# Buffers, banks and order at the stage borders of an encoder step

## The chip, the cores and the metric

The kernel runs on one core of a Trainium2 chip. The metric is the time of one execution in microseconds (us) on the device; the kernel before took 2932.59 us, the median of three runs (2931.63 to 2932.82). The engines are TensorE (PE, with its weight loads PEld), VectorE (DVE), ScalarE (ACT), GpSimd (POOL) and SyncE (SP), which here only issues DMAs. Each engine works off its own queue of instructions in a fixed order; where an instruction waits, everything behind it in that queue waits too.

## The reference

One layer of a streaming encoder, for a new stream of 2048 frames (16 tiles of 128 rows) and for the next 16 frames of 8 running streams (one more tile, the samples', number 16):

```python
def encoder_layer(x, ...):
    h = rmsnorm(x, g_mix_pre)
    y, new_k, new_v, new_conv = parallel_mixer(h, ...)   # band attention | conv, then w_out
    x = x + rmsnorm(y, g_mix_post)
    h = rmsnorm(x, g_mem_pre)
    x = x + rmsnorm(memory_attention(h, mk, mv, w_mq, w_mo), g_mem_post)
    h = rmsnorm(x, g_ffn_pre)
    f = (silu(h @ w_gate) * (h @ w_up)) @ w_down
    x = x + rmsnorm(f, g_ffn_post)
    return x, new_k, new_v, new_conv
```

The model width is 1024, the hidden width 2816, the memory has 256 tokens. All is fp32.

## The kernel before

Every large product is made of three matmuls on operands split into a high part (a cast to fp32r on ACT) and a low part (a subtraction on DVE or POOL). `mm3` (L271 to L273) does that for one output bank, `mm3h` (L279) for two halves of 512 columns. So each weight tile that is loaded costs an ACT cast and a DVE or POOL subtraction before TensorE can use it.

The stages run one after the other, but the instructions of neighbouring stages are mixed. A planner (the scheduler of the framework, which works with a timeline of its own at build time) writes the order of each engine's queue by the priority of the instructions, which is their order in the program. `high_priority(offset=n)` moves a block n places forward in that order, and `issue_after(ins)` makes those instructions of a block that run on the engine of `ins` come after it in that queue; instructions on other engines are not bound by it.

Memory is laid out by hand. `sbF` (fp32), `sbR` (fp32r, its last 20 KB per partition named `sbx` in the profile) and `ps` (the eight 2 KB banks of PSUM, `psb`) are areas of a fixed size, and `flexb` are pieces that come and go with a stage. A `Region` gives names to places in KB: `lay` puts buffers one behind the other, `at` at given offsets. Each name is a ring: the n-th tile of a name gets place n modulo the number of places. Two stages' names may lie on the same bytes, and then the later one waits until the earlier one's last reader is done.

The stages and what the change touches in them:

- Projection and convolution (`phase_proj`). The last group's norms (`late_norms`, `conv_norm`, L516 to L540) run inside the attention's first steps. Their normalised tile `xnx` lies after `thx` and `zx`, at 28 and 30 KB of `sbF`; the key output `ko` lies at 21 to 29 KB and is stored by L674.
- Attention (`attention`), 128 units of (head, tile). Near its end, `weigh` (L921) turns the row sums of tile 0 and tile 1 into reciprocals and transposes them, at the units named by `WEIGH`; the output weights are loaded by `out_weights`.
- Output projection (`mixout`), 17 tiles in the order samples, 0, 1, ... 15. `by_column(t)` (L935, POOL) spreads tile t's reciprocals into one buffer `rj`; `prep(t)` loads the convolution's part, multiplies with L979 (PE) and L982 (DVE), and splits the result into `mh` and `ml` (L988 ACT, L989 DVE). A tile's product takes 48 matmuls (L1017, helper L279) into two banks of the ring `y`. Then come squares (L1031), the scale (L1032, L288, L289 on POOL), L1035 (DVE, two halves, which frees the two banks and writes `po`), the residual add L1036 (POOL) and the store L1037. The ring `p` of banks serves `prep`, `weigh` and the transposes of the samples' work. That work is the whole memory attention of the samples' tile, a generator `cross_sample` which the loop advances by `RATE` steps after each second k from the tile number `FROM` on; its weights are split by L1075 (ACT) and L1076 (DVE), and it ends with `postnorm` (L324 to L330), which also takes `po`.
- Memory attention (`phase_cross`), 16 tiles: `norm(t)` (load of `xt`, L296, L288, L289, L303, transposes L306, split L307 and L308), `scores(t)` with the eight weights `f1`, softmax (L1209 to L1218), `probs(t)` (transposes L1224, split L1227 and L1228), `values(t)` with the eight weights `f2`, then `postnorm` (L328 on DVE, the add L329 and the store L330 on POOL). The weights go through the staging ring `stg` (`load`, L1188 SP, L1191 ACT, L1192 DVE or POOL). `natural(g, p)` (L1241 to L1264) takes a pair of finished tiles, normalises them (L1252, L1254 and L1255 on POOL, L1256 on DVE), makes sums and differences on POOL (L1257 to L1263) and stores seven forms in DRAM (`hn`). There are nine pairs (`PAIRS`), and the loop does at most one after each tile.
- Gate and up (`gate_up`), three groups of three pairs by 22 blocks of weights. `tform(g, j)` loads form j of a group (L1331, three loads), transposes it (L1334) and splits it (L1336 ACT, L1337 DVE). `wforms(f)` loads gate and up (L1343, L1344), makes sums on POOL (L1351 to L1354) and splits seven forms (L1356 ACT, L1357 DVE). Seven products of 12 matmuls (L1364) make one block. The first `wforms` and the seven first `tform` stand under `high_priority(offset=HP)`. What is left of the pairs is done here, one after each second block of group 0.
- Down (`down`) is not touched.

## Time and profile before

| | us |
|---|---|
| median of three runs | 2932.59 |
| the profiled execution | 2939.42 |
| its span, first to last instruction | 2937.6 |
| DVE busy | 2072.0 |
| ACT busy | 1306.7 |
| POOL busy | 1413.3 |
| transfers: mean over the span | 169 GB/s |

The profile is of one execution. PE's share of the span includes matmuls that ran at a lower clock, so a busy PE is not PE at its best. In a timeline row stand the start, the duration, the engine and line, the operation and its tiles, and in brackets how long the engine was idle before it and which instruction ended the wait. A row of a stretch gives the busy time of each engine with its count of instructions, then the granted clock of TensorE (1.00 is full speed), the share of DMA time and the rate.

### The profile page before, as it was taken

The numbers are of one execution on the slowest core, as the hardware profiler recorded it, in microseconds if no ns is written. First come the engines' busy times: TensorE is split into PE (matmuls) and PEld (weight loads), VectorE is DVE, ScalarE is ACT, GpSimd is POOL, SyncE is SP. The second block draws the span as 40 slices with busy tenths as digits, with TensorE's granted clock in tenths as the row PEclk, the third lists the DMA queues.
The fourth block names the chain that finished last, engine by engine and source line by source line (L and its number), as shares of the span: only waits on it lengthen the run. The fifth ranks groups of instructions, "written<-read, shape, count | busy, mean of one in ns | idle before, by whom it ended". The sixth has DMA issues, their size and how long they took to land.

```text
span 2937.6 us, 44541 instructions
## 1 busy us (share of the span) xinstructions
PE 2873.1 (98%) x16248; PEld 2594.9 (88%) x16248; DVE 2072.0 (71%) x3053; ACT 1306.7 (44%) x2623; POOL 1413.3 (48%) x1298
## 2 busy tenths in 40 slices
PE   9999999999999998999989999999999999999998
PEld 8999999988877677888879999999999998888786
DVE  7696885889983344344568888788788997555656
ACT  4444465678872233232334333433344444332433
POOL 1367496731133443153656555456556775424413
PEclk9999999999999999999999999999999999999999
DMA  8635253666535664132454333644344446656664
GB/s 289 245 106 189 80 179 116 207 225 219 209 116 188 234 209 136 57 132 93 158 181 163 116 134 120 206 161 157 130 150 142 143 143 226 222 172 227 224 216 142
DMA packets 200383, 496.81 MB, mean 169 GB/s; under 512 B 19258, under 2 KB 90810, under 8 KB 191323
## 3 DMA queue, kind: packets, MB, share of 16 engines
q1 hardware_dynamic: 186274, 426.98, 43.3%
q0 software_dynamic: 13888, 66.98, 6.1%
q8 instruction: 127, 2.08, 0.3%
q14 instruction: 94, 0.76, 0.1%
HBM read 362.82 MB, written 139.16 MB: 171 GB/s over the span
## 4 chain that ended last, share of the span: by engine, by line
PE 41%; DMA 4%; POOL 3%; DVE 3%; issue 2%; ACT 0%; SPq 0%; DVEq 0%; POOLq 0%; ACTq 0%
PE psb L273 13%; PE psb L272 13%; PE psb L271 13%; DMA sbf<-in_w_down_dram 2%; PE psb L279 1%; POOL sbf L1479 1%; DMA sbf<-x 1%; PE psb L1334 1%; DMA sbf<-in_w_gate_dram 0%; DVE sbr L1549 0%; DMA sbf<-hn 0%; DVE sbr L1357 0%; POOL sbf L329 0%; DVE sbx L1357 0%; DMA hn<-sbf 0%
## 5 line engine op out<-in xcount | busy, mean ns | idle before, releaser
L271 PE MATMUL psb<-sbr 128*128 128x384 f32 (+3 forms) x2672 | 916.5, 345 | 4.5 <-ACT sbr L1548 1.7
L272 PE MATMUL psb<-sbr 128*128 128x384 f32 (+3 forms) x2356 | 805.2, 342 | 0.5 <-DVE sbr L321 0.3
L273 PE MATMUL psb<-sbr 128*128 128x512 f32 (+2 forms) x1712 | 610.2, 358 | 3.7 <-DVE sbr L1549 3.6
L271 PEld LDWEIGHTS psb<-sbr 128*128 128x128 f32 x2672 | 503.8, 189 | 40.0 <-ACT sbr L1548 3.5
L273 PE MATMUL psb<-sbr,sbx 128*128 128x384 f32 (+2 forms) x1484 | 475.5, 322 | 1.6 <-POOL sbx L266 1.6
L272 PEld LDWEIGHTS psb<-sbr 128*128 128x128 f32 x2356 | 445.3, 189 | 27.4 <-DVE sbr L321 1.0
L273 PEld LDWEIGHTS psb<-sbr 128*128 128x128 f32 x1712 | 322.0, 188 | 39.7 <-DVE sbr L1549 7.5
L1357 DVE TENSOR_TENSOR sbr<-sbf,sbr 128x512 fp32r<-128x512 f32 x258 | 263.1, 1023 | 38.9 <-ACT sbr L1356 38.3
L273 PEld LDWEIGHTS psb<-sbr,sbx 128*128 128x128 f32 x1484 | 280.2, 189 | 1.9 <-POOL sbx L266 1.8
L1356 ACT CAST sbr<-sbf 128x512 fp32r<-128x512 f32 x258 | 159.1, 620 | 275.7 <-PE psb L272 232.2
L504 DVE SCALAR_TENSOR_TENSOR psb<-sbf,psb 128x768 f32<-128x768 f32 (+1 forms) x290 | 264.2, 911 | 6.2
L279 PE MATMUL psb<-sbr 128*128 128x512 f32 x984 | 244.2, 397 | 9.7 <-DVE flexb L1035 7.3
L279 PEld LDWEIGHTS psb<-sbr 128*128 128x128 f32 x984 | 184.0, 190 | 55.0 <-DVE flexb L1035 7.5
L1549 DVE TENSOR_TENSOR sbr<-sbf,sbr 128x384 fp32r<-128x384 f32 (+2 forms) x242 | 165.3, 707 | 93.9 <-ACT sbr L1548 92.9
L266 POOL TENSOR_TENSOR sbx<-sbf,sbr 128x1024 fp32r<-128x1024 f32 (+1 forms) x62 | 151.1, 2440 | 80.4 <-ACT sbr L264 70.5
L279 PE MATMUL psb<-sbr,sbx 128*128 128x512 f32 x750 | 186.7, 396 | 2.7 <-DVE sbx L989 1.8
L1479 POOL TENSOR_TENSOR sbf<-sbf 128x512 f32<-128x512 f32 x77 | 107.0, 1393 | 169.8 <-DMA sbf<-in_w_down_dram 168.1
L1548 ACT CAST sbr<-sbf 128x384 fp32r<-128x384 f32 (+2 forms) x242 | 112.6, 483 | 169.8 <-PE psb L272 145.9
L514 POOL TENSOR_TENSOR flexb<-flexb,flexb 128x128 f32<-128x128 f32 (+1 forms) x180 | 171.2, 952 | 20.5 <-ACT flexb L513 11.1
L271 PE MATMUL psb<-sbr,sbx 128*128 128x384 f32 (+1 forms) x524 | 170.9, 327 | 2.7 <-ACT sbx L1356 1.9
L279 PEld LDWEIGHTS psb<-sbr,sbx 128*128 128x128 f32 x750 | 139.6, 189 | 37.1 <-issue 3.3
L1356 ACT CAST sbx<-sbf 128x512 fp32r<-128x512 f32 x153 | 94.8, 620 | 165.0 <-PE psb L272 142.9
(328 smaller groups left out, 5903.4 us busy)
## 6 DMA issues: line engine op xcount, KB each, us to landing
af<-flexb SPq DMA_DIRECT2D x33, 1344.0 KB, 5.7
sbf<-in_w_down_dram SPq DMA_DIRECT2D x154, 256.0 KB, 3.5
sbf<-in_w_gate_dram SPq DMA_DIRECT2D x66, 512.0 KB, 3.4
sbf<-in_w_up_dram SPq DMA_DIRECT2D x66, 512.0 KB, 3.5
sbf<-af SPq DMA_DIRECT2D x85, 384.0 KB, 4.1
sbf<-x SPq DMA_DIRECT2D x49, 512.0 KB, 4.0
sbf<-in_w_in_dram SPq DMA_DIRECT2D x48, 512.0 KB, 3.9
sbr<-ks POOLq DMA_DIRECT2D x16, 1024.0 KB, 8.6
```

Of the source, the lines that this page charges most:

```text
L266: self.lo_engine.tensor_tensor(lo[:, c], wf[:, c], hi[:, c].bitcast(F32), ALU.subtract)
L271: nc.tensor.matmul(ps, lh, rh, start=start, stop=False, **kw)
L272: nc.tensor.matmul(ps, lh, rl, start=False, stop=False, **kw)
L273: nc.tensor.matmul(ps, ll, rh, start=False, stop=stop, **kw)
L279: nc.tensor.matmul(y[o], l, r[:, o * 512:(o + 1) * 512], start=start and x == 0, stop=stop and x == 2)
L504: nc.vector.scalar_tensor_tensor(acc if w < CW - 1 else o, src(w), cwt[:, j, w:w + 1], acc, ALU.mult, ALU.add)
L514: nc.gpsimd.tensor_tensor(o, o, v, ALU.add)
L1356: nc.scalar.copy(hs[j][:, :], src[j])
L1357: nc.vector.tensor_tensor(ls[j][:, :], src[j], hs[j][:, :].bitcast(F32), ALU.subtract)
L1479: nc.gpsimd.tensor_tensor(acc[:, :], acc[:, :], q[:, :], ALU.add if s > 0 else ALU.subtract)
L1548: nc.scalar.copy(ch[:, m], a[:, x, m])
L1549: nc.vector.tensor_tensor(cl[:, m], a[:, x, m], ch[:, m].bitcast(F32), ALU.subtract)
```

## The change

The diff does the following, border by border.

- Late norms: the two places of `xnx` are used in the reverse order, 30 KB first.
- Attention to output projection: tile 0 and tile 1 are weighed at units 117 and 122 instead of 122 and 124, and `by_column(0)` is done two units after the first, instead of at the start of `mixout`.
- Output projection: `y` has four banks and `p` two, instead of three and three; the samples' `postnorm` gets a buffer of its own, `spo`; `RATE` is 1.5 instead of 1.3; the samples' instructions that run on DVE are put behind the last split that `prep` has written so far.
- Memory attention: the staging ring has four places instead of three for the first twelve weights (eight `f1`, four `f2`), and three (`stg2`) for the rest; four `f2` weights instead of two are written ahead of the rest, now before the first `scores`, and no longer tied to its last exponential. `natural` runs behind the residual add of the same tile on POOL and no longer after the last tile, so that the pair (12, 14) moves into `gate_up`; its buffer `nt` moves to 22 KB there.
- Gate and up: other homes for weights (`wf`), sums (`s`) and loaded forms (`nat`, with nine places `nat0` for group 0 and five for the others instead of three), other homes for forms 4 and 5, another order of the banks for products, four banks instead of two for the transposes of group 0 (`tr0`), and `HP` 300 instead of 100.

```diff
@@ -34,17 +34,17 @@
 KL = PAST + DEC_S - 2 * KB
 EPS = 1e-6
 NEG = -1e30
-RATE = 1.3
+RATE = 1.5
 DEPTH = 2
-WEIGH = (122, 124)
+WEIGH = (117, 122)
 FROM = 2
-F2 = 2
+F2 = 4
 MID = 4
 TR0 = [12, 8]
 MM = [12, 14, 4, 6]
 LATE = 15
 WARM = (6, 0, 6)
-HP = 100
+HP = 300
 HP2 = 200
 
 GROUPS = [[[0, 1, 2], [3, 4, 5]], [[6, 7, 8], [9, 10, 11]], [[12, 13, 14], [15, S_TILE]]]
@@ -172,7 +172,7 @@
                    .at("qhx", 1.5, (fa, [17.5]), (fb, [6]), (sbF, [12, 13.5]))
                    .at("qlx", 1.5, (fa, [19]), (fb, [7.5]), (sbF, [15, 16.5]))
                    .lay(sbF, 18, ("vo", 1, 3), ("ko", 8, 1))
-                   .lay(sbF, 22, ("thx", 2, 1), ("zx", 2, 2), ("xnx", 2, 2))
+                   .lay(sbF, 22, ("thx", 2, 1), ("zx", 2, 2)).at("xnx", 2, (sbF, [30, 28]))
                 .lay(sbF, 44.75, ("us", 5.75, 1), ("cwt", 0.484375, 1), ("cvec", 0.0625, 1), ("half", 0.0625, 1))
                    .lay(fb, 0, ("ct", 3, 5), ("bst", 0.03125, 2), ("bmv", 0.03125, 2), ("ss", 0.03125, 6),
                         ("rstd", 0.03125, 6))
@@ -321,13 +321,14 @@
                     nc.vector.tensor_tensor(lo[:, sl, :], ps[:, :, :], hi[:, sl, :].bitcast(F32), ALU.subtract))
         return last
 
-    def postnorm(self, pool, y, xt, gbc, dst, dma=None, bufs=2):
+    def postnorm(self, pool, y, xt, gbc, dst, tag="po"):
         nc = self.nc
         r = self.rms(pool, y)
-        o = self.t(pool, [P, D], F32, "po", bufs)
+        o = self.t(pool, [P, D], F32, tag)
         nc.vector.scalar_tensor_tensor(o[:, :], y, r[:, :], gbc[:, :], ALU.mult, ALU.mult)
-        nc.gpsimd.tensor_tensor(o[:, :], o[:, :], xt[:, :], ALU.add)
+        added = nc.gpsimd.tensor_tensor(o[:, :], o[:, :], xt[:, :], ALU.add)
         nc.gpsimd.dma_start(dst, o[:, :])
+        return added
 
     def finish(self, pool, y, xt, gbc, dst, parts, engine):
 
@@ -895,6 +896,8 @@
             if i in WEIGH:
                 for _ in self.weigh(WEIGH.index(i), ps_t, "t"):
                     pass
+            if i == WEIGH[0] + 2:
+                self.by_column(0)
             if i in (n - 13, n - 11, n - 9, n - 7):
                 next(self.wo_load)
 
@@ -958,13 +961,13 @@
         sbF, sbR = self.sbF, self.sbR
         (ft, fr), ff = self.flex(ctx, (2048, F32), (2048, F32R)), self.fa
         pool = (Region().lay(sbF, 34.5, ("wf", 4, 3), ("gbc", 4, 1))
-                .at("ct", 2, (ff, [2, 10])).lay(ff, 0, ("an", 2, 1)).lay(ff, 5, ("po", 4, 1))
+                .at("ct", 2, (ff, [2, 10])).lay(ff, 0, ("an", 2, 1)).lay(ff, 5, ("po", 4, 1)).at("spo", 4, (ff, [22]))
                 .lay(ff, 12, ("junk", 2, 1), ("xt", 4, 2), ("sh", 8, 1), ("ss", 0.03125, 6), ("rstd", 0.03125, 6),
                      ("nmx", 0.03125, 1), ("sm", 0.03125, 1), ("ri", 0.03125, 1)).lay(ff, 26, ("sgain", 4, 1))
                 .at("mh", 4, (sbR, [40, 88])).at("ml", 4, (sbR, [44, 92]))
                 .lay(sbR, 96, ("sTh", 4, 1), ("sTl", 4, 1)).lay(ft, 0, ("sT", 8, 1))
                 .at("kvh", 4, (sbR, [64, 80]), (fr, [0])).at("kvl", 4, (sbR, [104, 84]), (fr, [4])))
-        ps_y = ps_p = ps_so = Region().lay(self.ps, 0, ("y", 2, 3), ("p", 2, 3), ("so", 4, 1))
+        ps_y = ps_p = ps_so = Region().lay(self.ps, 0, ("y", 2, 4), ("p", 2, 2), ("so", 4, 1))
         for _ in self.wo_load:
             pass
         ws, self.w = self.wo, pool
@@ -986,7 +989,7 @@
             ml = self.t(pool, [P, KC, P], F32R, "ml", 2)
             for sl, src in ((slice(4, 8), ct[:, :, :]), (slice(0, 4), att)):
                 nc.scalar.copy(mh[:, sl, :], src)
-                nc.vector.tensor_tensor(ml[:, sl, :], src, mh[:, sl, :].bitcast(F32), ALU.subtract)
+                self.last_prep = nc.vector.tensor_tensor(ml[:, sl, :], src, mh[:, sl, :].bitcast(F32), ALU.subtract)
             ready[t] = (mh, ml)
 
         def ahead(i):
@@ -1003,8 +1006,6 @@
         ready = {}
         with self.tc.high_priority(offset=HP2):
             for t in order[:2]:
-                if t != S_TILE:
-                    self.by_column(t)
                 prep(t)
         fill, steps, due = iter(()), 0, 0.0
         for i, t in enumerate(order):
@@ -1019,7 +1020,8 @@
                     next(pre, None)
                     due += RATE if i >= FROM else 0.0
                     while due >= 1:
-                        next(fill, None)
+                        with self.tc.issue_after(self.last_prep.ins):
+                            next(fill, None)
                         due -= 1
             for _ in pre:
                 pass
@@ -1162,13 +1164,14 @@
         yield from dense(oT, "w_mo", y)
         xt = self.t(pool, [P, D], F32, "xt", 2)
         nc.sync.dma_start(xt[:, :], self.x1[S_TILE])
-        self.postnorm(pool, flat(y), xt, gpost, self.x2[S_TILE], bufs=1)
+        self.postnorm(pool, flat(y), xt, gpost, self.x2[S_TILE], "spo")
 
     def phase_cross(self, ctx):
         nc, A = self.nc, self.A
         sbF, sbR = self.sbF, self.sbR
         fr = Joined(*self.flex(ctx, *[(1024, F32R)] * 11))
-        pool = (Region().lay(sbF, 0, ("stg", 4, 3), ("gpre", 4, 1), ("junk", 2, 1), ("hn", 4, 1), ("xt", 4, 3))
+        pool = (Region().lay(sbF, 12, ("gpre", 4, 1), ("junk", 2, 1), ("hn", 4, 1), ("xt", 4, 3))
+                .at("stg", 4, (sbF, [0, 4, 8, 30])).at("stg2", 4, (sbF, [0, 4, 8]))
                 .lay(sbF, 34.5, ("gpost", 4, 1), ("z", 4, 2), ("po", 4, 1), ("ss", 0.015625, 6),
                      ("rstd", 0.015625, 6), ("nmx", 0.03125, 2), ("sm", 0.03125, 2), ("ri", 0.03125, 2))
                 .at("sh", 4, (sbR, [96, 44, 24])).at("sl", 4, (sbR, [100, 52, 28]))
@@ -1183,8 +1186,8 @@
         gpre = self.gain(pool, "g_mem_pre", "gpre")
         gpost = self.gain(pool, "g_mem_post", "gpost")
 
-        def load(src, tag, engine=nc.vector):
-            wf = self.t(pool, [P, D], F32, "stg")
+        def load(src, tag, engine=nc.vector, stage="stg"):
+            wf = self.t(pool, [P, D], F32, stage)
             nc.sync.dma_start(wf[:, :], src)
             wh = self.t(pool, [P, D], F32R, tag + "h", 1)
             wl = self.t(pool, [P, D], F32R, tag + "l", 1)
@@ -1210,8 +1213,8 @@
             z = self.t(pool, [P, MH, NM], F32, "z", 2)
             sm = self.t(pool, [P, MH], F32, "sm", 2)
             for h in range(MH):
-                self.last_exp = nc.scalar.activation(z[:, h, :], sv[:, h, :], AF.Exp, bias=nmx[:, h:h + 1],
-                                                     accum_out=sm[:, h:h + 1])
+                nc.scalar.activation(z[:, h, :], sv[:, h, :], AF.Exp, bias=nmx[:, h:h + 1],
+                                     accum_out=sm[:, h:h + 1])
             ri = self.t(pool, [P, MH], F32, "ri", 2)
             nc.vector.reciprocal(ri[:, :], sm[:, :])
             for h in range(MH):
@@ -1234,7 +1237,7 @@
                 if t == NPT - 2 and k == MID:
                     self.last_probs = probs(z)
                 self.mm3h(halves(y), ph[:, k, :], pl[:, k, :], f2[k][0], f2[k][1], k == 0, k == KC - 1)
-            self.postnorm(pool, y[:, :, :].rearrange("p a b -> p (a b)"), xt, gpost, self.x2[t], bufs=1)
+            return self.postnorm(pool, y[:, :, :].rearrange("p a b -> p (a b)"), xt, gpost, self.x2[t])
 
         gffn = self.gain(Region().at("gffn", 4, (self.gffn, [0])), "g_ffn_pre", "gffn")
 
@@ -1269,30 +1272,26 @@
         f1 = [load(self.f1s[:, k, :, :].rearrange("p h n -> p (h n)"), f"f1{k}",
                    nc.gpsimd if k in (1, 3, 5) else nc.vector) for k in range(KC)]
         hq[1] = norm(1)
+        f2 = [load(self.f2s[:, k, :], f"f2{k}") for k in range(F2)]
         z = scores(*hq[0][1:], "y")
-        f2 = []
-
-        def more(n, event):
-            with self.tc.issue_after(event.ins):
-                for k in range(len(f2), min(len(f2) + n, KC)):
-                    f2.append(load(self.f2s[:, k, :], f"f2{k}"))
-
-        more(F2, self.last_exp)
         for t in range(NPT):
             pp = probs(z) if t < NPT - 1 else self.last_probs
             if t == 0:
-                more(KC, self.last_split)
+                with self.tc.issue_after(self.last_split.ins):
+                    f2 += [load(self.f2s[:, k, :], f"f2{k}", stage="stg2") for k in range(F2, KC)]
             if t + 1 < NPT:
                 z = scores(*hq[t + 1][1:])
             if t + 2 < NPT:
                 hq[t + 2] = norm(t + 2)
-            values(t, hq.pop(t)[0], *pp)
+            added = values(t, hq.pop(t)[0], *pp)
             for g, p in list(todo):
                 ready = all(x == S_TILE or x < t for x, _ in PAIRS[g][p][:2])
-                if ready and t >= 4:
-                    natural(g, p)
+                if ready and 4 <= t < NPT - 1:
+                    with self.tc.issue_after(added.ins):
+                        natural(g, p)
                     todo.remove((g, p))
                     break
+        pool.at("nt", 4, (sbF, [22]))
         self.todo = todo
 
     def shift_caches(self, name, s):
@@ -1310,16 +1309,17 @@
         sbF, sbR = self.sbF, self.sbR
         t6h, t6l, w8, fx, af0, af1 = self.flex(ctx, (1536, F32R), (1536, F32R), (1024, F32R), (1536, F32), (2688, F32),
                                                (2688, F32))
-        pool = (Region().at("wf", 4, (sbF, [12, 18, 46.5, 22]))
-                .at("s", 2, (sbF, [26, 28, 38.5])).at("nat", 2, (sbF, [40.5, 42.5, 44.5]))
+        pool = (Region().at("wf", 4, (sbF, [12, 18, 26, 42.5]))
+                .at("s", 2, (sbF, [8, 10, 38.5])).at("nat", 2, (sbF, [0, 2, 4, 6, 40.5])).at("nat0", 2, (sbF, [0, 2, 4, 6, 40.5, 12, 14, 18, 20]))
                 .at("x1", 1.5, (sbF, [30, 31.5])).at("x2", 1.5, (sbF, [33, 34.5]))
                 .at("x3", 1.5, (sbF, [36]), (fx, [0])).at("th", 1.5, (fx, [1.5, 3, 4.5]))
                 .at("wh", 2, (sbR, [68, 72, 76, 80, 84, 88, 92, 104]), (w8, [0]))
                 .at("wl", 2, (sbR, [70, 74, 78, 82, 86, 90, 94, 106]), (w8, [2]))
                 .at("af", 10.5, (af0, [0]), (af1, [0])).at("t6h", 6, (t6h, [0])).at("t6l", 6, (t6l, [0])))
-        for j, (oh, ol) in enumerate(((0, 6), (12, 18), (56, 62), (24, 30), (36, 42), (48, 96))):
+        for j, (oh, ol) in enumerate(((0, 6), (12, 18), (56, 62), (24, 30), (36, 96), (42, 48))):
             pool.at(f"t{j}h", 6, (sbR, [oh])).at(f"t{j}l", 6, (sbR, [ol]))
-        ps_mm = ps_tr = Region().at("mm", 2, (self.ps, [8, 10, 0, 2, 4, 6])).at("tr", 2, (self.ps, [12, 14]))
+        ps_mm = ps_tr = (Region().at("mm", 2, (self.ps, [0, 2, 4, 6, 8, 10])).at("tr", 2, (self.ps, [12, 14]))
+                         .at("tr0", 2, (self.ps, [12, 14, 8, 10])))
         ts = [None] * 7
 
         def tform(g, j):
@@ -1327,9 +1327,9 @@
             lo = self.t(pool, [P, 4, 3 * P], F32R, f"t{j}l")
             for p in range(3):
                 n = PAIRS[g][p][2]
-                x = self.t(pool, [P, 512], F32, "nat")
+                x = self.t(pool, [P, 512], F32, "nat" if g else "nat0")
                 nc.sync.dma_start(x[:n, :], self.hn[g][:n, p, TFORM[j], :])
-                ps = self.t(ps_tr, [P, 4, P], F32, "tr")
+                ps = self.t(ps_tr, [P, 4, P], F32, "tr" if g else "tr0")
                 for k in range(4):
                     nc.tensor.transpose(ps[:, k, :n], x[:n, k * P:(k + 1) * P], self.ident[:n, :n])
                 c = slice(p * P, p * P + n)
```

## The prediction

> **What bounds the kernel now.** I read the page first, then the busy time by stretches, the list of what TensorE waited for, and the order of time around each place where it stood still.
>
> ```profile
> span 2937.6 us, 44541 instructions
> PE 2873.1 (98%) x16248; PEld 2594.9 (88%) x16248; DVE 2072.0 (71%) x3053; ACT 1306.7 (44%) x2623; POOL 1413.3 (48%) x1298
> ```
>
> TensorE is busy 2873.1 of 2937.6 us, and the change takes no matmul away. It can win only TensorE's idle time and the half-speed matmuls after it. So I looked for both at the borders between stages.
>
> ```profile
> 841.00:876.00 35.00, 30.18 (x161) 24.50 (x160) 27.33 (x45) 20.37 (x41) 11.15 (x10) 0.95 0.46 151
> 1105.00:1112.00 7.00, 0.05 (x1) 0.00 (x0) 1.40 (x2) 1.08 (x2) 5.39 (x7) 0.70 0.43 151
> 1143.00:1149.00 6.00, 4.31 (x26) 3.30 (x25) 5.79 (x6) 3.96 (x11) 0.00 (x0) 1.00 0.55 175
> 1505.00:1520.00 15.00, 10.59 (x65) 8.84 (x63) 11.71 (x13) 8.27 (x16) 11.09 (x12) 1.00 0.73 235
> 1520.00:1532.00 12.00, 7.27 (x35) 5.89 (x35) 3.92 (x8) 3.67 (x7) 5.54 (x7) 0.82 0.75 261
> 1532.00:1538.00 6.00, 6.00 (x19) 6.00 (x20) 4.92 (x6) 2.57 (x5) 5.32 (x5) 0.51 0.42 152
> 1538.00:1544.00 6.00, 6.00 (x39) 5.93 (x39) 4.42 (x6) 2.66 (x5) 4.39 (x3) 1.00 0.57 188
> 1870.00:1880.00 10.00, 7.91 (x51) 7.36 (x50) 6.51 (x12) 4.53 (x8) 3.50 (x3) 1.00 0.72 245
> ...
> 875.00:1105.00 230.00, 230.00 (x1170) 168.96 (x1169) 93.11 (x144) 72.69 (x173) 90.72 (x102) 1.00 0.62 210
> 1150.00:1490.00 340.00, 336.99 (x1595) 280.18 (x1594) 158.22 (x168) 107.08 (x233) 142.20 (x170) 1.00 0.32 110
> ...
> 1540.00:1870.00 330.00, 329.17 (x1921) 328.07 (x1920) 274.85 (x372) 132.81 (x244) 195.81 (x145) 1.00 0.41 145
> ```
>
> The columns are the stretch, its length, the busy time of PE, PEld, DVE, ACT and POOL, the granted clock, DMA share and GB/s. Length less PE is idle: 4.82 into the output projection, 6.95 at its end, 1.69 at the first memory attention, 4.41 + 4.73 = 9.14 into gate and up, 2.09 at its first change of group, 3.01 inside the memory attention, nothing inside the output projection. At 1532 to 1538 the granted clock is 0.51, and 19 matmuls run where 39 run in the next 6 us: about 3 us more.
>
> **The end of the output projection: four "y" banks and the own row buffer.**
>
> ```profile
> 1098.67 5.61 PE L279 MATMUL psb<-sbr 128*128 128x512 f32 x24
> ...
> 1112.32 8.44 PE L279 MATMUL psb<-sbr 128*128 128x512 f32 x24 [7.27 <-DVE flexb L1035]
> ...
> 1104.86 3.25 POOL L329 TENSOR_TENSOR flexb<-flexb 128x1024 f32<-128x1024 f32 x1 [7.84 <-DVE flexb L328]
> ...
> 1108.44 0.63 POOL L330 DMA_DIRECT2D x<-flexb  x1
> ...
> 1111.51 1.41 DVE L1035 SCALAR_TENSOR_TENSOR flexb<-psb,flexb,sbf 128x512 f32<-128x512 f32 x2 [5.60 <-DMA x<-flexb]
> ```
>
> Three banks serve two halves per tile, so the second half of the last tile reuses a bank of the tile before, which L1035 must empty. L1035 writes "po", and that one buffer still holds the samples' row until its store (L330) has left. So TensorE stands 7.27 us, and the 24 matmuls then take 8.44 instead of 5.61: 2.83 more. With four banks the last tile reuses those of two tiles back, and with "spo" L1035 does not wait for the store either. All 7.27 + 2.83 = 10.10 can go. What is late next is the first scores: their weights are split into places that the projection's weights leave, and TensorE comes 10 us sooner.
>
> ```profile
> 1123.95 1.05 ACT L1191 CAST sbr<-sbf 128x1024 fp32r<-128x1024 f32 x1 [0.81 <-DMA sbf<-f1s]
> ```
>
> That split waits for its load. Four staging buffers instead of three bring loads forward, and the freed last tile releases its weights from its first matmuls on. I take 9.0 of 10.1; the bounds are 0 (the loads do not move) and 10.1. The samples' work at RATE 1.5 instead of 1.3 is the same work sooner: nothing, as the stretch from 875 is full.
>
> TensorE's half clock after the pause is a rule of the Trainium skill too (TensorE: Matmul & The Clock Gate, "What's actually happening"): about 3.4 us of idleness halve the clock, about 3.4 us of work restore it. By that each pause would cost 1.7 us beside itself, an estimate; the rows say 2.83 and 3, and they count.
>
> **The start of the memory attention.** Four value weights split before the first softmax, not two behind its exponential, take splits out of the chain. Its 1.69 idle waits for transposed probabilities, which four splits don't shorten, but the scores come apart. I take 0.7, between 0 and 1.7.
>
> **Into gate and up: other homes, priority 300, no 'natural' at the end.**
>
> ```profile
> PE psb L1334 <- DMA sbf<-hn: 4.5, 2, 3.5
> PE psb L271 <- ACT sbx L1356: 1.9, 1, 1.9
> PE psb L1334 <- DVE sbr L1337: 1.8, 3, 1.0
> ...
> 1509.15 3.03 DVE L1256 SCALAR_TENSOR_TENSOR sbf<-sbf,flexb 128x1024 f32<-128x1024 f32 x1
> ...
> 1513.53 9.71 SPq L1331 DMA_DIRECT2D sbf<-hn  x5
> ...
> 1531.24 1.26 POOL L1352 TENSOR_TENSOR sbf<-sbf 128x512 f32<-128x512 f32 x1 [6.44 <-DMA sbf<-in_w_gate_dram]
> ...
> L1337 DVE TENSOR_TENSOR sbr<-psb,sbr 128x512 fp32r<-128x512 f32 x15 | 10.0, 685 | 13.3 <-ACT sbr L1336 13.3
> ```
>
> Three causes, each met by an edit. The 21 loads of the first forms (L1331) go through three buffers that lie on the softmax's tiles: 4.5 us. Nine buffers on the old staging area can be filled before. The second pair of weights (L1352) waits for a home under "po" (46.5) and "xt" (22); the new homes 26 and 42.5 are free earlier: 1.9. The pair (12, 14) of 'natural' stands in DVE's queue between the forms (L1256): 1.8; it moves into gate and up. Form 4 leaves the place of the last probabilities, so only forms 5 and 6 need the last values; they come 60 matmuls in. Idle 9.14 and 3 of slow clock make 12.1, and at 0.82 over 12 us up to 2.2 more: 14.3. I take 12.0, bounds 3 (below) and 14.3.
>
> The price is the pair moved. Its two L1256 and four adds (L1257 to L1263) now meet a stage in which DVE is busy 274.85 of 330 us:
>
> ```profile
> L1256 DVE SCALAR_TENSOR_TENSOR sbf<-sbf,flexb x18: 1276/1284/3417, 1255.9 to 1551.4; 128x1024 f32<-128x1024 f32 x16, 64x1024 f32<-64x1024 f32 x2
> ...
> L1257 POOL TENSOR_TENSOR sbf<-sbf x9: 1255/1285/1665, 1265.6 to 1552.8; 128x512 f32<-128x512 f32 x8, 64x512 f32<-64x512 f32 x1
> ```
>
> That is 2 x 1.28 to 2 x 3.42 on DVE and 4 x 1.29 on POOL, against DVE's idle 55 us in 22 steps, 2.5 each. It is spread over two or three steps; I charge 1.2, bounds 0 and 6.8 (all of the worst on the path).
>
> A rule of the Trainium skill speaks against this move (SBUF — State Buffer, "Who interferes with whom"): a DVE instruction with two SBUF inputs and a GpSimd one that reads SBUF block each other whole. The spread from 1276 to 3417 agrees. By it the four adds hold DVE for 5.2 us beyond its own 2.6, 7.8 as an estimate, and if none of it were covered the sum would lose 6.6 more.
>
> **Into the output projection: (117, 122), the early product of tile 0, DVE order.**
>
> ```profile
> 867.82 1.05 ACT L1075 CAST flexb<-sbf 128x1024 fp32r<-128x1024 f32 x1 [2.85 <-DMA sbf<-in_w_mq_dram]
> ...
> 868.95 1.23 DVE L1076 TENSOR_TENSOR flexb<-sbf,flexb 128x1024 fp32r<-128x1024 f32 x1 [2.24 <-ACT flexb L1075]
> ...
> 872.15 1.28 DVE L989 TENSOR_TENSOR sbx<-flexb,sbx 128x512 fp32r<-128x512 f32 x2
> ...
> 872.89 3.41 PE L279 MATMUL psb<-sbr,sbx 128*128 128x512 f32 x8 [1.76 <-DVE sbx L989]
> ```
>
> Splits of the samples' weights (L1076, two of 1.2 us) stand on DVE before tile 0's (L989), which TensorE waits for. 'issue_after' puts them behind it: 1.76 idle goes, and with it 3.41 - 8 x 5.61/24 = 1.54 of slow matmuls. ACT's cast (L1075) is not moved, so its 2.85 can remain. I take 3.3, bounds 0 and 4.82 + 1.54 = 6.4.
>
> **Smaller places.** The late norms wait for a store of the keys that lies under their buffer; with the order turned the first lies elsewhere:
>
> ```profile
> 614.03 0.81 DVE L528 TENSOR_SCALAR sbf<-psb,flexb 128x512 f32<-128x512 f32 x1 [1.44 <-DMA out_dram<-sbf]
> ...
> PE psb L532 <- DVE sbf L528: 1.6, 1, 1.6
> ```
>
> I take 1.2 of 1.6. Inside the memory attention 'natural' goes ahead of the residual add:
>
> ```profile
> 1302.67 1.28 DVE L328 SCALAR_TENSOR_TENSOR sbf<-psb,sbf 128x1024 f32<-128x1024 f32 x1 [3.33 <-POOL sbf L289]
> ...
> 1307.10 0.19 POOL L1254 TENSOR_SCALAR sbf<-sbf 128x1 f32<-128x1 f32 x1 [4.46 <-ACT sbf L1252]
> ...
> 1307.90 2.39 POOL L329 TENSOR_TENSOR sbf<-sbf 128x1024 f32<-128x1024 f32 x1
> ```
>
> L328 ends at 1303.95, the add starts at 1307.90, and the next norm's "xt" is free only after it. With the add first: 2.0 of the 3.01. The change of group has more load buffers but the same two banks: 0.5 of 2.09.
>
> **Two "p" banks for three.** A bank is held for little more than
>
> ```profile
> L982 DVE TENSOR_TENSOR flexb<-sbf,psb 128x512 f32<-128x512 f32 x15 | 10.2, 683 | 15.3 <-PE psb L979 15.3
> ...
> L979 PE MATMUL psb<-sbr 128*128 128x512 f32 x13 | 5.4, 414 | 0.0
> ```
>
> 0.41 + 0.68 us, a few times in a tile of 15 us. I charge 1.0 in all, bounds 0 and the last rival.
>
> **Sum.** 9.0 + 0.7 + 12.0 + 3.3 + 1.2 + 2.0 + 0.5 - 1.2 - 1.0 = 26.5 us. The profiled execution took 2939.4 (1.8 of it outside the span) and would take 2912.9; the median of the three runs is 6.8 lower, so 2932.6 - 26.5 = 2906.1.
>
> **The rivals.**
> One handover gives nothing. Either the first scores wait for their weights (9.0 back), or priority 300 puts five to nine forms on DVE ahead of the last probabilities: 0.685 each, 3.4 to 6.2, and 3 of clock, up to 9. For it: the split above waits for its load, and 21 forms and 7 splits fill DVE there. Against: four buffers. 2906.1 + 9 = 2915, to 2923 with small losses: 0.20. Both: 2924: 0.08.
> The edits do not reach the chip: instruction order follows the planner's clock, and each wait moves to the next in line. Within 6 us of before, 0.04; against it, the buffers and banks are places, not order.
> Slower: the two "p" banks. Products, weights' turns and the samples' turns share them, and TensorE takes them in order; a third request waits. Without that charge the gain is 27.5, so from 27.5/15 = 1.8 us a tile over 15 tiles it is used up. At 2.5 us, two holds of 1.1 and a queue behind the splits, it is 37.5: 2942.6. For it: the samples' DVE work now stands behind 'prep'. Against: no idle in the 230 us of that stage. 0.07.
> More than forecast, above 35 us: 0.03.
>
> **How the numbers follow.** The forecast, a gain of 18 to 35, has 0.58. The range 2896 to 2922 holds it, most of the 0.20 and a little of the last: 0.8. Faster by over 0.2% (5.9 us, about what a measurement can tell) is 0.58 + 0.20 + 0.03 and 0.05 of the 0.08: 0.86. Same: 0.04 + 0.03 = 0.07. Slower: 0.07.
>
> **What would show it.** The 7.27 before L279 and the clock of 0.51 are gone; L1334 no longer waits for hn; L989 runs before L1076; stretches as long as 1505 to 1538 show no more than 2 us idle. A wait of L279 for L1191/L1192, or idle time inside the output projection at L979 or L1057, would prove me wrong.

## The result, and the profile after

| | median, us | lowest to highest | runs |
|---|---|---|---|
| before | 2932.11 | 2930.31 to 2932.82 | 4 |
| after | 2916.14 | 2912.2 to 2917.7 | 4 |

The ratio is 0.9944, 95% interval [0.9927, 0.9962]: 16 us faster (11 to 21), where 26.5 were forecast. The profiled execution of after took 2912.2 (span 2910.4), the fastest of its four, and that of before 2939.4, 7 above its median; so the two profiles lie 27.2 apart, more than the medians, and places are compared here, not spans.

The page of after, its first lines:

```profile
span 2910.4 us, 44563 instructions
PE 2859.6 (98%) x16248; PEld 2589.3 (89%) x16248; DVE 2081.8 (72%) x3053; ACT 1308.3 (45%) x2623; POOL 1400.0 (48%) x1298
```

Busy time by stretches of after, the columns as in the prediction (stretch, length, PE, PEld, DVE, ACT, POOL, granted clock, DMA share, GB/s):

```profile
839.00:874.00 35.00, 32.32 (x175) 26.48 (x174) 23.58 (x36) 19.95 (x36) 11.54 (x10) 1.00 0.45 143
874.00:1089.00 215.00, 212.69 (x1105) 157.71 (x1104) 90.18 (x140) 68.77 (x164) 84.20 (x102) 0.99 0.64 220
935.00:950.00 15.00, 12.74 (x83) 7.81 (x75) 8.21 (x17) 3.66 (x10) 6.47 (x8) 0.89 0.85 282
1089.00:1104.00 15.00, 15.00 (x72) 12.51 (x71) 13.29 (x10) 7.63 (x11) 11.81 (x8) 1.00 0.64 215
1126.00:1133.00 7.00, 5.12 (x30) 3.84 (x29) 5.55 (x5) 4.25 (x12) 0.75 (x2) 1.00 0.00 0
1133.00:1473.00 340.00, 340.00 (x1620) 283.94 (x1619) 157.92 (x171) 106.84 (x233) 137.23 (x170) 1.00 0.33 114
1473.00:1573.00 100.00, 91.09 (x527) 87.96 (x525) 82.31 (x99) 42.65 (x80) 67.83 (x60) 0.98 0.50 180
1573.00:1820.00 247.00, 247.00 (x1432) 246.90 (x1431) 200.98 (x273) 94.29 (x171) 143.42 (x103) 1.00 0.34 125
1820.00:1850.00 30.00, 29.40 (x186) 27.98 (x185) 24.92 (x39) 16.33 (x32) 11.74 (x10) 1.00 0.72 240
2440.00:2450.00 10.00, 7.44 (x27) 5.67 (x26) 9.84 (x14) 3.77 (x8) 7.22 (x7) 0.83 0.80 254
```

The end of the output projection (1089 to 1104) and the inside of the memory attention (1133 to 1473) are full. Inside the projection 2.3 us of idle time and a clock of 0.89 have come up, at 935 to 950. The first change of group begins at 1812 in a full stretch and has 0.60 idle in 1820 to 1850. Most of what is left stands in 1473 to 1573, the way into gate and up with its first blocks: 8.91 idle, and about 2 us for a clock of 0.98. The list of what TensorE waited for in after (in total, times, the longest) says for what:

```profile
PE psb L271 <- DVE flexb L1407: 6.3, 2, 5.4
...
PE psb L271 <- DVE sbf L1396: 2.3, 1, 2.3
PE psb L1097 <- DMA sbf<-in_cache_mem_kT_dram: 2.3, 3, 1.7
...
PE psb L271 <- DVE sbf L1407: 1.2, 1, 1.2
...
PE psb L533 <- DVE sbf L529: 0.3, 1, 0.3
```

L1334 is gone from it: the first forms no longer wait for their loads. L1396 is new, and L1407 has 6.3 and 1.2 where before had 2.1: DVE empties the banks of the first blocks too late (L1407 also has 0.9 at 2217, outside the border). Into the output projection, and at its end, the timeline of after shows:

```profile
866.73 1.20 PE L279 MATMUL psb<-sbr,sbx 128*128 128x512 f32 x4 [1.36 <-ACT sbx L991]
...
866.97 1.29 DVE L992 TENSOR_TENSOR sbx<-flexb,sbx 128x512 fp32r<-128x512 f32 x2
...
1095.64 8.78 PE L279 MATMUL psb<-sbr 128*128 128x512 f32 x38
```

L992 is the old L989; it now runs ahead of every split of the samples' weights (the old L1076, from 886 on). The product waits 1.36 for the cast instead. At the end 38 matmuls run without a pause.

One place that the change does not touch became longer, the way into down. Before, by stretches:

```profile
2465.00:2480.00 15.00, 12.94 (x60) 10.40 (x59) 13.81 (x20) 5.81 (x13) 9.05 (x8) 1.00 0.80 255
```

2.06 idle at full clock before; 2.56 idle, and 1.7 us for a clock of 0.83, after.

The two executions also differ in clock where no edit explains it. The row of before:

```profile
545.00:625.00 80.00, 75.26 (x473) 71.55 (x471) 65.63 (x119) 48.27 (x128) 49.58 (x76) 0.96 0.75 249
```

The clock of this stretch is 1.00 in after, but 0.98 in the profile of the same kernel run again, and 1.00 in before with only the border of gate and up changed. At 0.96 it costs before about 3 us, so a term read from one execution is good to some 2 or 3 us.

### The profile page after: what moved, and what is told of

The parts are those of the page before. It is cut to its first block, busy times and chain, and to the rows that moved or that the text cites. A ratio compares the mean times of both kernels' runs of the same rounds, so it can differ in the third digit from the quotient of the medians.

```text
span 2910.4 us, 44563 instructions
## 1 busy us (share of the span) xinstructions
PE 2859.6 (98%) x16248; PEld 2589.3 (89%) x16248; DVE 2081.8 (72%) x3053; ACT 1308.3 (45%) x2623; POOL 1400.0 (48%) x1298
## 4 chain that ended last, share of the span: by engine, by line
PE 81%; DVE 5%; DMA 5%; POOL 3%; issue 3%; ACT 2%; SPq 0%; DVEq 0%; POOLq 0%; ACTq 0%
PE psb L273 18%; PE psb L272 18%; PE psb L271 18%; PE psb L279 18%; DMA sbf<-in_w_down_dram 2%; PE psb L848 2%; PE psb L817 2%; PE psb L835 1%; POOL sbf L1479 1%; PE psb L1334 1%; DMA sbf<-x 1%; POOL flexb L515 1%; PE psb L1097 1%; DMA sbf<-in_x_prompt_dram 1%; DVE flexb L732 1%
## 5 line engine op out<-in xcount | busy, mean ns | idle before, releaser
L273 PE MATMUL psb<-sbr 128*128 128x512 f32 (+2 forms) x1712 | 609.1, 357 | 4.7 <-DVE sbr L1549 4.6
L273 PE MATMUL psb<-sbr,sbx 128*128 128x384 f32 (+2 forms) x1484 | 474.5, 321 | 1.6 <-POOL sbx L266 1.6
L273 PEld LDWEIGHTS psb<-sbr 128*128 128x128 f32 x1712 | 321.0, 188 | 40.2 <-DVE sbr L1549 8.2
L1357 DVE TENSOR_TENSOR sbr<-sbf,sbr 128x512 fp32r<-128x512 f32 x258 | 258.1, 1003 | 48.2 <-ACT sbr L1356 45.0
L273 PEld LDWEIGHTS psb<-sbr,sbx 128*128 128x128 f32 x1484 | 279.9, 189 | 1.9 <-POOL sbx L266 1.8
L279 PE MATMUL psb<-sbr 128*128 128x512 f32 x984 | 241.2, 395 | 1.4 <-DVE sbr L266 0.5
L279 PEld LDWEIGHTS psb<-sbr 128*128 128x128 f32 x984 | 182.6, 189 | 45.2 <-issue 4.3
L279 PE MATMUL psb<-sbr,sbx 128*128 128x512 f32 x750 | 184.6, 394 | 1.7 <-ACT sbx L991 1.4
L1357 DVE TENSOR_TENSOR sbx<-sbf,sbx 128x512 fp32r<-128x512 f32 x153 | 165.9, 1087 | 14.9 <-ACT sbx L1356 14.6
L279 PEld LDWEIGHTS psb<-sbr,sbx 128*128 128x128 f32 x750 | 138.7, 188 | 36.0 <-issue 4.5
```

The source lines that it names most:

```text
L273: nc.tensor.matmul(ps, ll, rh, start=False, stop=stop, **kw)
L279: nc.tensor.matmul(y[o], l, r[:, o * 512:(o + 1) * 512], start=start and x == 0, stop=stop and x == 2)
L1357: nc.vector.tensor_tensor(ls[j][:, :], src[j], hs[j][:, :].bitcast(F32), ALU.subtract)
```

## The experiments

All times are medians beside runs of before on the same chip (medians 2936.7 to 2938.2 there), and gains are differences of medians; the intervals are those of the ratio. Eight kernels ran on one chip in two rounds; the two with the adds on DVE and the one with the pair (12, 14) back on a second, the pairs taken apart on a third. Kernels of different chips are compared by their ratios.

| kernel | us | ratio to before, 95% interval |
|---|---|---|
| after again | 2918.86 | 0.9932 [0.992, 0.9945] |
| before + row buffer + four y banks | 2924.28 | 0.9956 [0.9944, 0.9969] |
| before + row buffer | 2926.65 | 0.9966 [0.9953, 0.9978] |
| before + four y banks | 2934.58 | 0.9989 [0.998, 0.9997] |
| before + the border of gate and up | 2938.35 | 0.9997 [0.9988, 1.0007] |
| after, pairs written later | 2917.36 | 0.9929 [0.9916, 0.9941] |
| after, pairs held | 2921.26 | 0.9947 [0.9933, 0.9961] |
| after, samples at 1.3 | 2922.07 | 0.9945 [0.9932, 0.9957] |
| after, adds on DVE | 2913.31 | 0.9912 [0.9897, 0.9927] |
| after, held, adds on DVE | 2913.55 | 0.9916 [0.9902, 0.9929] |
| after, pairs taken apart | 2916.67 | 0.9923 [0.991, 0.9937] |
| after, pair (12, 14) back | 2938.80 | 1.0004 [0.9995, 1.0013] |

"Block" in the expectations means a round of two blocks of weights (`fp`).

**After again.** The same kernel, as a measure for the others.

> The changed kernel once more, as the yardstick of the others. If the difference between the two profiled executions (27.2 us) is the true one and the first four runs were unlucky: about 2906. If the median of 16 us less is right and the profiled execution of the kernel before was a slow one of its kind: 2916, give or take 2, and the runs of the kernel before stay within 2930 to 2933 at a clock above the 0.993 of that profile.

It gained 18.7 us here. The runs of before lay between 2934.1 and 2941.0, not within 2930 to 2933 as expected, so an execution of 2939.4 is no unusual one here.

**Row buffer and banks, together and each alone**, put into before:

```
-    ...lay(ff, 5, ("po", 4, 1))
+    ...lay(ff, 5, ("po", 4, 1)).at("spo", 4, (ff, [22]))      # row buffer; the samples' postnorm takes "spo"
-    ("y", 2, 3), ("p", 2, 3)
+    ("y", 2, 4), ("p", 2, 2)                                  # banks
```

> The kernel before with only the four y banks (two p banks) and the samples' own row buffer. Theory 'the bank was the wait': the 7.27 us before L279 and the 2.83 us of slow matmuls after it go, 2932 - 10 = 2922, and no idle time of TensorE over 1 us appears in the first scores. Rival 'the weights of the first scores are late next': TensorE waits there for L1191 or L1192 instead, and 2928 to 2932 remains. Rival 'two p banks': idle time at L979 or L1057 in the projection, over 2932.

> Before, with the samples' last row in its own buffer and nothing else (three y banks). Theory that the two edits at this place are substitutes: L1035 no longer waits for the store (5.60), so the 7.27 before the last L279 falls below 2 us, the clock stays above 0.9, and the gain is 8 to 12 us, nearly all of the 13 that buffer and banks gave together. Rival, they add up: the bank of the tile before is still being emptied when the last tile's second half comes, a gap of 3 us or more stays, gain 3 to 6 us.

> Before, with four y and two p banks and nothing else (the samples' row still in the shared buffer). Theory of substitutes: the last tile finds a free bank, no gap before the last L279, but L1035 still waits 5.6 us for the store, so that x1 of the last tile comes later; the first scores don't need it, gain 8 to 12 us. Rival: the late L1035 holds a bank that the first scores need, and 2 to 5 us of idle come up there; gain 5 to 8 us. If two p banks cost time inside the projection, it shows here as idle between 875 and 1098 that before did not have (0.0).

Together they gave 13.3 us, 9 to 16 by the interval, and TensorE waits nowhere between 1090 and 1120. The row buffer alone gave 10.4. Its timeline:

```profile
1100.95 1.41 DVE L1035 SCALAR_TENSOR_TENSOR flexb<-psb,flexb,sbf 128x512 f32<-128x512 f32 x2 [1.00 <-POOL flexb L289]
...
1101.76 5.78 PE L279 MATMUL psb<-sbr 128*128 128x512 f32 x24 [0.19 <-DVE flexb L1035]
```

Of 7.27 us 0.19 are left, with three banks: L1035 no longer waits for the store, and the bank is empty in time. The banks alone gave 2.5 us, less than either theory said. The pause moved to the first scores (timeline):

```profile
1110.23 1.04 ACT L1191 CAST sbr<-sbf 128x1024 fp32r<-128x1024 f32 x1 [4.40 <-DMA sbf<-f1s]
...
1113.27 1.02 ACT L307 CAST sbx<-psb 128x1024 fp32r<-128x1024 f32 x1
...
1114.34 2.08 PE L279 MATMUL psb<-sbr,sbx 128*128 128x512 f32 x4 [5.13 <-ACT sbx L307]
```

The cast that the scores need (L307) stands on ACT behind the split of a weight whose load is late. So the row buffer carries this handover, four banks add at most a few us to it, and two "p" banks cost nothing that shows: 215 us of projection had 0.8 idle there.

**The border of gate and up alone**, put into before:

```
-HP = 100
+HP = 300
-                if ready and t >= 4:
+                if ready and 4 <= t < NPT - 1:
-    "wf", 4, (sbF, [12, 18, 46.5, 22])   "nat", 2, (sbF, [40.5, 42.5, 44.5])
+    "wf", 4, (sbF, [12, 18, 26, 42.5])   "nat0", 2, (sbF, [0, 2, 4, 6, 40.5, 12, 14, 18, 20])
...
```

> The kernel before with only the border into gate and up: other homes, nine places for the first forms, four transpose banks, priority 300, the pair (12, 14) of 'natural' moved into the first blocks. Theory 'the moved pair is paid back': the idle 9.1 us and the slow clock at 1532 to 1538 go (about -13), and idle time of about 9 us comes in the first four blocks, before L271 behind L1396 and L1407: 2932 - 4 = 2928. Rival 'the pair is hidden and the payback comes from elsewhere': 2919, and the idle time in the first blocks stays under 2 us.

No gain that shows (2938.35 against 2937.55; -2 to 3.5 us by the interval). TensorE's waits from 1490 to 1860 (lines are two higher here):

```profile
PE psb L271 <- DVE flexb L1409: 5.4, 1, 5.4
PE psb L271 <- DVE sbf L1398: 3.0, 1, 3.0
PE psb L271 <- DVE sbf L1409: 1.2, 1, 1.2
```

The waits of the entry are gone, and 9.6 us in the first blocks stand in their place.

**The pairs written later**, in rounds 4 and 7 of group 0:

```
-                    if g == 0 and x == 1 and self.todo:
+                    if g == 0 and x == 1 and fp in (4, 7) and self.todo:
```

> The changed kernel with the two pairs of 'natural' left to gate and up done after the blocks of fp 4 and 7 instead of fp 0 and 1; the same work, only later. Theory 'two pairs in the first two steps are too much for DVE and POOL, which also catch up with the first forms': the idle 8.9 us at L271 in the first four blocks shrink to under 3 and little comes at the later places: 2916 - 6 = 2910. Rival 'a pair costs its price wherever it stands, since the two engines block each other': the idle time moves to the later blocks, 2916.

Same time, and TensorE's longest wait from 1480 to 1830, 4.1 us for L1407, is still in the first blocks. It comes at 1543.6, and the first L1259 (the old L1256) at 1505.4. The planner had drawn the pairs forward to the same place, so nothing was tested.

**The pairs held**: the same, with both pairs really behind their round.

```
+    added = self.act_forms(af, g)
+    if g == 0 and fp in (4, 7):
+        with self.tc.issue_after(formed.ins), self.tc.issue_after(added.ins):   # formed: L1421
+            self.natural(*self.todo.pop(0))
```

> After, with the two pairs of 'natural' that stand in gate and up tied behind the last product form and the last add of blocks 4 and 7, so that they really run there (170 instructions later on DVE). Theory: the idle of the first four blocks (2.32 at L1396, 1.20 and 5.40 at L1407, 8.9 us) is the price of the pairs, which meet the weights' adds on POOL and the backlog of the first forms on DVE. Then those three gaps fall to 2 us or less in all, at blocks 4 and 7 no more than 2 us appear, and the time is about 7 us below after (ratio to before near 0.991, after had 0.9932). Rival 1: the backlog of the first forms alone makes the idle: 6 us or more of it stay, time within 2 us of after. Rival 2: a pair costs the same wherever it stands: 2 to 5 us of idle in each of blocks 4 and 7, time as after.

By stretches:

```profile
1480.00:1580.00 100.00, 100.00 (x590) 97.71 (x589) 75.76 (x107) 45.39 (x84) 52.82 (x40) 1.00 0.43 147
...
1660.00:1690.00 30.00, 24.90 (x129) 24.26 (x128) 25.07 (x26) 9.21 (x17) 19.00 (x18) 0.89 0.54 203
1690.00:1790.00 100.00, 97.01 (x553) 96.69 (x552) 81.87 (x107) 37.06 (x69) 66.08 (x54) 0.98 0.39 139
```

The first blocks are full, so the backlog of the first forms makes no idle time. The pairs took it along: 5.10 and 2.99 where they stand now, with the clock at 0.89 and 0.98 (rival 2). No gain; the median is even 2.4 us above that of after again, with overlapping intervals.

What a pair does there, in the timeline of after:

```profile
1554.41 1.29 POOL L1351 TENSOR_TENSOR sbf<-sbf 128x512 f32<-128x512 f32 x1 [0.62 <-DVE sbx L1357]
1555.65 0.57 POOL L1267 DMA_DIRECT2D hn<-sbf  x1
1556.24 1.28 POOL L1352 TENSOR_TENSOR sbf<-sbf 128x512 f32<-128x512 f32 x1
1557.47 1.26 POOL L1353 TENSOR_TENSOR sbf<-sbf 128x512 f32<-128x512 f32 x1
1558.69 1.26 POOL L1354 TENSOR_TENSOR sbf<-sbf 128x512 f32<-128x512 f32 x1
...
1556.63 3.87 DVE L1357 TENSOR_TENSOR sbx<-sbf,sbx 128x512 fp32r<-128x512 f32 x1
1560.43 0.54 DVE L1407 TENSOR_TENSOR flexb<-sbf,psb 128x384 f32<-128x384 f32 x1
...
1561.02 0.69 PE L271 MATMUL psb<-flexb,sbr 128*128 128x384 f32 x1 [5.40 <-DVE flexb L1407]
```

One L1357, 0.68 us when nothing is beside it, lasts 3.87 here: it begins 0.4 after the start of L1352 and ends 0.6 after the end of L1354. Behind it on DVE stands L1407, which empties the bank that TensorE needs. These three adds are those of the weights, not the pair's. The two smaller waits of after are nearer to the pair itself: ahead of the 2.32 at 1517 DVE takes turns with the pair's own adds (L1260, L1262, L1264), and ahead of the 1.20 at 1541 stands the pair's own L1259, 3.38 us long.

The long splits belong to the pairs. Of the 462 splits L1357 of gate and up none lasts over 3 us in before; each of the ten kernels with the new border has one to four, 14 in all, and each of the 14 begins 0.4 to 1.8 us after POOL has issued one of a pair's stores (here L1267). So the pair may do it by making both queues late, or by its stores on POOL, ahead of the run of adds. No experiment moved the stores, and which of the two it is stays open.

**The pairs' adds on DVE**, in rounds 0 and 1 and, in a second kernel, held in 4 and 7:

```
-            nc.gpsimd.tensor_tensor(tt[:, 0, :], xb[:, 0, :], xa[:, 0, :], ALU.subtract)
+            add.tensor_tensor(tt[:, 0, :], xb[:, 0, :], xa[:, 0, :], ALU.subtract)
...
-                        self.natural(*self.todo.pop(0))
+                        self.natural(*self.todo.pop(0), add=nc.vector)
```

> After, with the four adds of each of the two pairs in gate and up on DVE instead of POOL; the pairs stay in blocks 0 and 1. Theory, the price of a pair is what its adds do on POOL (they come ahead of the next weights' adds L1351 to L1354, and these then lock DVE's L1357 for up to 4.4 us): with 5.2 us less on POOL and 4 x 0.68 = 2.7 us more on DVE per pair, the idle of the first four blocks falls from 8.9 to 4 us or less, ratio to before 0.991 to 0.9925. Rival, the price is DVE's own load (83% busy in this stage): 2.7 us more on DVE per pair makes the idle 11 to 14 us, ratio 0.994 to 0.996.

> After, with both pairs tied to blocks 4 and 7 and their adds on DVE. No idle in the first four blocks, as when they were held with their adds on POOL. There the pairs cost 4.80 and 2.99 us at their new place. Theory of POOL: 2 us or less each, together under 3, time 5 us below after. Theory of DVE's load: 4 to 6 us each, time 2 to 4 us above after.

With the adds on DVE in rounds 0 and 1, ratio 0.9912; the 8.9 us are 6.8, of which 6.0 in one wait (timeline):

```profile
1544.50 5.94 DVE L1357 TENSOR_TENSOR sbr<-sbf,sbr 128x512 fp32r<-128x512 f32 x1
...
1550.96 0.69 PE L271 MATMUL psb<-flexb,sbr 128*128 128x384 f32 x1 [5.98 <-DVE sbf L1407]
```

So the theory of POOL was right in the sign (DVE's own load would have made it more) and wrong in the size: five adds of the products and the weights (L1447, L1448, L1352, L1353, L1449) still close DVE out. Held, the two pairs cost this (TensorE's waits):

```profile
PE psb L271 <- DVE flexb L1407: 5.5, 2, 2.8
```

2.75 each, between the theories, for 4.80 and 2.99 with the adds on POOL. Both kernels come out some 5 us below after again, the lowest of all, but on another chip, and their intervals overlap with its own.

**The pairs taken apart**: one DVE instruction of a pair in each of twelve blocks, tied behind L1421, adds on DVE.

```
+    if g == 0 and f >= 6:
+        with self.tc.issue_after(formed.ins):
+            if next(rest, True) and self.todo:
+                rest = self.pieces(*self.todo.pop(0), add=nc.vector)
+                next(rest)
```

> After, with the two pairs of gate and up taken apart: adds on DVE, and one DVE instruction of a pair (1.28 or 0.68 us) in each of twelve steps from step 7 on, each tied behind the step's last product form. Theory, what a pair costs is its standing in one step: DVE is idle 55 us in the 22 steps of a group, 2.5 each, and a pair brings 5.3 at once; one instruction a step fits. Then neither the 8.9 us of the first four blocks nor the 2.75 + 2.75 of the held pairs appear (together under 1.5 us), the time is 4 to 6 us below the held pairs with adds on DVE (ratio near 0.9895) and the lowest of all. Rival, DVE has no room for anything before the product forms that empty banks: about 0.5 us in each of the twelve steps, 5 us or more in all, ratio 0.991 to 0.992 as with the held pairs.

Ten of the twelve blocks show no idle time, two show 2.5 us each, 5.0 together, and the ratio is 0.9923: the theory of bunching falls, and the rival's even spread too. In four of the twelve a split (L1357) lasted 5.4 to 6.8 us, and in two of these it reached TensorE. The first of the two (timeline; lines are up to eleven higher: L1367 is L1357, L1418 is L1407):

```profile
1680.38 1.03 POOL L1461 TENSOR_TENSOR flexb<-flexb 128x384 f32<-128x384 f32 x1
1681.35 1.01 POOL L1462 TENSOR_TENSOR flexb<-flexb 128x384 f32<-128x384 f32 x1
1682.32 1.28 POOL L1361 TENSOR_TENSOR sbf<-sbf 128x512 f32<-128x512 f32 x1
1683.56 1.00 POOL L1463 TENSOR_TENSOR flexb<-flexb 128x384 f32<-128x384 f32 x1
1684.53 1.28 POOL L1362 TENSOR_TENSOR sbf<-sbf 128x512 f32<-128x512 f32 x1
1685.78 1.28 POOL L1363 TENSOR_TENSOR sbf<-sbf 128x512 f32<-128x512 f32 x1
...
1680.88 6.73 DVE L1367 TENSOR_TENSOR sbx<-sbf,sbx 128x512 fp32r<-128x512 f32 x1
...
1690.09 0.44 PE L271 MATMUL psb<-flexb,sbr 128*128 128x384 f32 x1 [2.50 <-DVE sbf L1418]
```

DVE did one add of 0.68 us more in this block, and a split was shut out by six adds in a row, none of them the pair's. The pair's store L1269 was issued 1.1 us before this split. The price of a pair is not its work but such a meeting.

**The pair (12, 14) back** behind the last tile:

```
-                if ready and 4 <= t < NPT - 1:
+                if ready and t >= 4:
```

> After, with the pair (12, 14) back behind the last tile of the memory attention, as in before, and one pair left in gate and up. Theory, a pair costs 3 to 5 us in gate and up and less at the border, where TensorE waits anyway: the idle of the first four blocks falls to 3 to 5 us, the way into gate and up gets 2 to 4 us of idle back, time 0 to 4 us below after. Rival, as forecast, the pair costs 1.2 us in gate and up and 1.8 or more at the border: time 0.6 us or more above after, up to 5 with a slow clock.

All of the gain is gone. Not DVE's queue but the loads did it (TensorE's waits, then the timeline):

```profile
PE psb L1334 <- DMA sbf<-hn: 19.9, 3, 15.1
```

```profile
1496.05 0.59 POOL L1261 DMA_DIRECT2D hn<-sbf  x1 [1.10 <-DVE sbf L1259]
...
1499.04 4.25 SPq L1331 DMA_DIRECT2D sbf<-hn  x2
...
1501.85 1.09 PE L1334 MATMUL psb<-ident,sbf 128*128 128x128 f32 x4 [15.12 <-DMA sbf<-hn]
```

The pair's tiles `na` and `nb` lie at 0 to 8 KB, where the first four of the new load buffers lie. So the load L1331 stands on SP until the store L1261 has read `na`. Neither theory had this: moving the pair is the condition for the new homes, not an edit of 1.8 beside them.

**The samples at 1.3**:

```
-RATE = 1.5
+RATE = 1.3
```

> After, with the samples' steps at 1.3 a product again, as in before, instead of 1.5. Theory: the small waits at L1097 for cached keys (0.4 to 1.7 us in all between 935 and 950), which before did not have, come from the faster rate; they go, and the time is 0 to 1.5 us below after. Rival: the rate decides nothing here, or the slower rate leaves samples' work for the end of the stage: time within 1 us of after or 1 to 3 above.

The waits for cached keys (2.3 us) go, and others come: 3.2 us above after again by the medians, the way of the rival, though the intervals overlap. Its timeline at the first scores:

```profile
1107.76 1.04 ACT L1194 CAST sbr<-sbf 128x1024 fp32r<-128x1024 f32 x1 [3.24 <-DMA sbf<-f2s]
```

TensorE waits 4.3 us for L307 behind it on ACT, as with the banks alone. Only the rate differs from after, so it is the rate that moved the late load here; by what path was not followed.

## Why the prediction came out as it did

The sign was right and the forecast 10 us too low: the 16 us lie just below the gain of 18 to 35 that it named, the 18.7 just inside. Its terms, by the places of the two profiled executions:

| term | forecast | measured | how |
|---|---|---|---|
| end of the projection | 9.0 | 10.1 | 7.27 and 2.83 both gone; 13.3 in time, run alone |
| start of the memory attention | 0.7 | -0.2 | idle 1.69, now 7 - 5.12 = 1.88 |
| into gate and up, less the pair | 10.8 | 4.2 | idle 9.14 + 0.83 and 5.1 of clock, now 8.91 and 2.0; this border run alone: no gain in time that shows |
| into the projection | 3.3 | 3.9 | idle 4.82, now 2.68; clock 0.95, now 1.00, over 35 us |
| late norms | 1.2 | 1.3 | 1.6, now 0.3 |
| 'natural' behind the add | 2.0 | 3.0 | 3.01, now 0 |
| change of group | 0.5 | 1.5 | 2.09, now 0.60 |
| two "p" banks; samples' rate | -1.0; 0 | 0; -4.0 | 215 - 212.69, all at L1097, and 1.7 for the clock of 0.89 |
| way into down | not named | -2.2 | 2.06 idle, now 2.56 and 1.7 of clock |
| sum | 26.5 | 17.6 | measured in time: 16 (11 to 21) and 18.7 (16 to 23) |

The two executions themselves lie 27.2 apart; the rest stands at places that the table doesn't have, some 3 of it in the clock of 545 to 625. That the sum comes near the medians is therefore no proof of each term.

**The step that failed** is the price of the moved pair: "It is spread over two or three steps; I charge 1.2, bounds 0 and 6.8". I had divided DVE's idle time by the steps (2.5 us each) and set the pair's work against it. The way in itself gave more than the 12.0 charged for it: its idle 9.14 and its 5.1 of clock are gone. The price was 8.91 - 0.83 = 8.1, and 2 of clock. The runs show that work against room is the wrong sum: without pairs the first blocks have no idle time (100.00 of 100.00 busy), with the two that stand there now 8.91, and in the run with the pairs taken apart a block with 0.68 us more work lost 2.5. The one pair that stood there before shows at most 0.83, behind a border at which TensorE waited anyway. The upper bound of 6.8 was too low too, since it counted the pair's own instructions and not the one next to them.

The sentence on the Trainium skill (SBUF — State Buffer, "Who interferes with whom") gave 6.6 more to lose, a sum of 19.9; its estimate for the pair was 7.8. The size agrees with the 8.1 of the trace; what blocks agrees only in part. The pair's own adds stand beside DVE ahead of the wait of 2.32, but the largest wait has the weights' adds beside it, and with the pair's adds moved off POOL a split still stood 5.94 us.

**Right as named:** 7.27 and the clock of 0.51 gone, L1334 free of `hn`, L989 ahead of L1076. L279 did not wait for the weights, and no idle time at L979 or L1057 came up. "No more than 2 us in stretches like 1505 to 1538" was wrong. At the end of the projection the mechanism was right, but I named the banks first, and the row buffer does four fifths of it alone. The change of group was taken at 0.5 because its two banks stay; 1.5 of its 2.09 went, so the load buffers decided most of it, or the new order of banks: not separated.

**The rivals.** "One handover gives nothing" (2915) has the time, but not by its two ways. The wait of the first scores for their weights did not come in after, though it did with the banks alone and at the rate 1.3, so that risk was real. Forms ahead of the last probabilities cost nothing. The planner's rival (order follows its own clock) is false for the change as a whole and true of one experiment, the pairs written later. Two "p" banks did not slow the projection.

**Open:** why the way into down lost 2.2 us. The wait ahead of its L273 was 2.56 to 2.84 in after and eight of the kernels with the new border, 1.33 in one (held, adds on DVE), and 1.47 or 1.48 in all without it. And which of the small edits saved the 3.0 inside the memory attention was read from the order of the queues, not tried alone. Nor was a pair tried with its stores issued by another engine than POOL.

## What to carry to other kernels

When work moves into a stage where DVE and POOL are both busy, don't set its microseconds against the idle time of the engine; look for the instruction that frees TensorE's next bank, and at what POOL runs in a row while the instruction ahead of it on DVE reads two operands from SBUF. Before an edit is priced by itself, see whether its buffers lie under another edit's: the pair and the new load buffers were one edit. And look in the trace for a moved piece before you read its time: a place in the program is not a place in the queue.

## What the runs showed of the hardware

A DVE instruction with two operands in SBUF was shut out for 3.87 to 6.75 us while POOL ran three to six adds back to back at 0.98 to 1.30 us each, as when nothing is beside them. The Trainium skill (SBUF — State Buffer, "Who interferes with whom") has it that such an instruction and a GpSimd one reading SBUF contend, and one with at most one SBUF input does not. The trace agrees on the second point: L1407, which reads one operand from PSUM, took 0.54 throughout. But the wait is not bounded by one instruction of the other engine. In other steps DVE comes in between (after, timeline):

```profile
1703.30 1.28 POOL L1353 TENSOR_TENSOR sbf<-sbf 128x512 f32<-128x512 f32 x1
...
1703.52 1.61 DVE L1357 TENSOR_TENSOR sbr<-sbf,sbr 128x512 fp32r<-128x512 f32 x1
```

There L1357 waits for one add, 0.93 more than alone. At 1525.7 of after a split took 1.77, and POOL's adds beside it took 1.60 to 1.77 too: the engines took turns. In both places no store was issued by POOL in the 6 us before, and in each of the 14 long cases one was, at most 1.8 us before. That this decides was not tried.

The other surprise is how far single executions lie apart: the same kernel took 2912.2 to 2921.2 over nine of them (four beside the first result, five as after again), with the clock granted over the whole span between 0.995 and 0.997. That is half the gain, so no stage was judged by the span of one.
